# Turning round the one-hot products of an expert-weight matrix: which operand stays, which one moves

## The chip, the cores and the metric

The kernel runs on one core of a Trainium2 chip. The metric is the device time in microseconds (us). Three runs of the kernel before took 2843.61, 2845.25 and 2845.64 us, with 2845.25 us as the median.

## The reference, cut to what matters

The program is one transformer layer for 256 prompt tokens and 64 sample tokens: differential attention, a gated chunk MLP, memory attention, an output projection, and then a PEER layer, in which every token picks 128 of 16384 experts. The change is in the PEER layer, which the reference writes with gathers:

```
s = jnp.einsum('thpc,hpkc->thpk', q, sub_keys)      # two sets of 128 keys per head
s1, i1 = lax.top_k(s[:, :, 0], 16); s2, i2 = lax.top_k(s[:, :, 1], 16)
...                                                 # the best 16 of the 256 sums, per head
g = softmax(top_s)
a = gelu(einsum('td,thkd->thk', xb, expert_u[eidx]))
out = einsum('thk,thkd->td', g * a, expert_v[eidx])
```

An expert's number is first key times 128 plus second key. Each token has 8 heads times 16 picks, so 128 slots, each with a first key, a second key and a weight.

## The kernel before, in words

For the 256 prompt tokens (`DN`) the kernel doesn't gather. It multiplies the tokens with every expert's row of `peer_u` (the pieces `Up`, 128 of them, each two loads of 512 KB and 48 matmuls at line 413), passes the result through Gelu, weights it with a dense matrix G (experts by tokens, nearly all zeros), and multiplies that with every row of `peer_v` (the pieces `Down`). For the 64 sample tokens the rows are gathered by indirect DMAs on POOL (`gathers`, lines 1502 to 1526), 64 gathers of `pur` and 64 of `pvr`, 1 MB each, into two or three buffers; each is used by one DVE instruction of 2048 elements (`dot`, `axpy`).

G is built while the `Up` pieces run, in 32 units of eight tokens (`TU`), one every two or three pieces (`weights_lane`, lines 1339 to 1359). Such a unit is `g_unit` (lines 1447 to 1475). With slots on the 128 partitions, DVE compares an index table `io` (the number i at every place [i, t]) with the tokens' first keys, and again with their second keys: two one-hot tables in bf16, each 128 keys by 8 tokens with the tokens innermost (`oa`). The weight of a slot is kept as three bf16 parts (`w0`, `w1`, `w2`), so that nothing of its 32 bits is lost, and DVE multiplies the second key's one-hot table by each part (`ob`). Then TensorE makes a 128 by 128 block of G for each token: the first key's one-hot rows of this token stay in the array, and the second key's weighted rows move through it, once for each part, summed in PSUM. Token k's rows are `oa[:, 0, :, k]` and `ob[:, j, :, k]`, so both operands are read in steps of eight bf16 elements, 16 bytes. The products of the first two parts are issued at line 1461; the third goes through the helper at line 271 (`mm`). ACT copies four tokens' blocks at a time into `st`, and a DMA on SP's queue writes 16 tokens to DRAM (`gd`), from where `weights_in` loads them after all units are done.

Float32 work goes through a stream: SP's queue loads `raw`, ACT rounds it into `hi`, DVE takes the rest into `lo`, and three float32r matmuls per block follow at line 413. The buffers of this stream are a ring of four to six.

The order of all engines' instructions is fixed when the program is built, by a small planner (class `Plan`, lines 123 to 249). It keeps a clock for each engine, adds a modelled cost for each instruction (`pe_cost`, `act_cost`, `dve_cost`, `pool_cost`), and lets a task issue its next step when the plan's PE clock has reached the time at which its inputs are due. The first two products of a token add 0.067 us each to the plan's PE clock; the third costs what `pe_cost` says for bf16, 0.0133 us and 128 columns at 2.4 per ns, which is 0.067 us too. `dve_cost` counts a bf16 output at half the time per element.

Of the kernel before, what the change touches and what calls it, by code (L numbers as in the profile page):

```python
# [14 lines left out]
BF16 = mybir.dt.bfloat16  # L15
AF = mybir.ActivationFunctionType
ALU = mybir.AluOpType
# [28 lines left out]
TU = 8  # L46
# [17 lines left out]
class Slots:  # L64
# [10 lines left out]
    def take(self):  # L75
        t, i = self.free.pop(0)
        x = self.make(i)
        self.used[id(x)] = (i, x)
        self.plan.touch(x, t, True)
        return x  # L80
# [171 lines left out]
def size(ap):  # L252
    n = 1
    for k in ap.shape[1:]:
        n *= k
    return n
# [34 lines left out]
def pe_cost(op, a, k):  # L291
    n = size(a[2]) / (2.4e3 if op == "matmul" and a[2].dtype == F32R else 0.6e3)
    if op == "matmul" and a[2].dtype == BF16:
        return 0.0133 + size(a[2]) / 2.4e3
    return max(0.107, n + 0.0133) if op == "matmul" else 0.216


# [4 lines left out]
def dve_cost(op, a, k):  # L302
    out = a[0] if a else k["out"]
    n = size(a[1]) if op == "tensor_reduce" else size(k["in_"]) if op == "max" else \
        size(k["in_values"]) if op in ("max_index", "match_replace") else size(out)
    return 0.16 + n / 0.96e3 * (6.2 if op == "reciprocal" else 0.5 if out.dtype == BF16 else 1)


def pool_cost(op, a, k):
# [9 lines left out]
def hybrid_kernel(ctx: ExitStack, tc: tile.TileContext, ins, outs, stop=None):  # L319
    nc = tc.nc  # L320
    plan = Plan()
    act, dve = Engine(plan, "act", nc.scalar, act_cost), Engine(plan, "dve", nc.vector, dve_cost)
    pool, pe = Engine(plan, "pool", nc.gpsimd, pool_cost), Engine(plan, "pe", nc.tensor, pe_cost)
    sync = Engine(plan, "sync", nc.sync, None)
    take, need, mark, spawn, step = plan.take, plan.need, plan.mark, plan.spawn, plan.step
    mm = pe.matmul
# [856 lines left out]
    R = {}  # L1183
# [155 lines left out]
    def weights_lane():  # L1339
        yield from need(*[("dec", i) for i in range(3)])  # L1340
        rtmp.close()
        q = open_pool(gtmp, "gtmp")
        R["io"] = q.tile([128, 128, TU], BF16, name="io")
        pool.tensor_copy(R["io"], cst[:, C_IO:C_IO + 128, None].to_broadcast([128, 128, TU]))
        OA = Slots(plan, q, "oa", [128, 2, 128, TU], BF16, 2)
        OB = Slots(plan, q, "ob", [128, 3, 128, TU], BF16, 2)
        ST = Slots(plan, q, "st", [128, 128, TB], F32, 2)
        st = None
        for t0 in range(0, DN, TU):
            yield from need(("up", GE0 + (GEN - GE0) * t0 // DN))  # L1350
            if t0 % TB == 0:
                st, = yield from take(ST)
            oa, ob = yield from take(OA, OB)
            spawn(g_unit(t0, oa, ob, OA, OB, ST, st))
        while len(gdone) < DN // TU:
            yield
        gtmp.close()
        open_late()
        mark("G")
# [86 lines left out]

    def g_unit(t0, oa, ob, OA, OB, ST, st):

        col = lambda nm: R[nm][:, None, t0:t0 + TU].to_broadcast([128, 128, TU])
        dve.tensor_tensor(oa[:, 0], R["io"], col("k0"), op=ALU.is_equal)  # L1450
        dve.tensor_tensor(oa[:, 1], R["io"], col("k1"), op=ALU.is_equal)
        yield
        for j in range(3):
            dve.tensor_tensor(ob[:, j], oa[:, 1], col(f"w{j}"), op=ALU.mult)
            yield
        for a in range(TU // 4):
            bk, = yield from take(BK)
            for k in range(4 * a, 4 * a + 4):
                o = bk[:, 128 * (k % 4):128 * (k % 4) + 128]
                for j in range(2):  # L1460
                    nc.tensor.matmul(o, oa[:, 0, :, k], ob[:, j, :, k], start=j == 0, stop=False)  # L1461
                    plan.clk["pe"] += 0.067
                mm(o, oa[:, 0, :, k], ob[:, 2, :, k], start=False, stop=True)
            yield
            o = t0 % TB + 4 * a
            act.activation(st[:, :, o:o + 4], bk.rearrange("p (t i) -> p i t", t=4), AF.Copy)
            BK.give(bk)
        OA.give(oa)
        OB.give(ob)
        if o == TB - 4:  # L1470
            plan.see(st)
            yield
            sync.dma_start(gd[t0 // TB][:, :128 * TB], st.rearrange("p i t -> p (i t)"))
            ST.give(st)
        gdone.append(t0)
# [393 lines left out]
```

## Time and profile before

| | us |
|---|---|
| median of three runs | 2845.25 |
| the profiled execution's own time | 2845.33 |
| its span, first to last instruction | 2843.6 |
| time outside the span | 1.7 |
| PE busy | 2788.7 |
| DVE busy | 1870.9 |
| ACT busy | 1101.7 |
| POOL busy | 472.7 |
| bytes moved by DMA | 634.75 MB |

A row of the profile's groups has the line and engine, the operation, the tiles (output, then inputs), the shapes and how often it ran; then the busy time of all in us and the mean of one in ns; then the idle time of the engine before it and what ended it. Matmuls are pipelined: one's duration is longer than its distance from the next, so distances are read from the chain of waits. [...]

The span has three stretches that matter here: everything up to the end of the routing (until 1365 us), the `Up` pieces with the building of G among them (1365 to 2005 us) and their last pieces (to 2104 us), and the `Down` pieces (to 2844 us).

### The profile page before, as it was taken

What the parts mean: (1) busy time and instruction counts of PE and PEld (TensorE: products, weight loads), DVE (VectorE), ACT (ScalarE), POOL (GpSimd) and SP (SyncE); (2) the same over time, 40 slices, a digit from 0 to 9 for tenths busy, and PEclk for the clock granted to TensorE, in tenths of its full rate; (3) what the DMA queues carried; (4) which work ended last, traced back from release to release, by engine and by line L of the source; (5) the groups of instructions that cost most, each with busy time, mean ns of one, the idle gap of its engine ahead of it and who ended that gap; (6) DMA issues with size and microseconds to landing.
All of it is one profiled execution on the core that took longest, in us unless ns stands there. A gap on an engine that the chain in (4) does not pass through costs nothing.

```text
span 2843.6 us, 42779 instructions
## 1 busy us (share of the span) xinstructions
PE 2788.7 (98%) x17350; PEld 2556.7 (90%) x17350; DVE 1870.9 (66%) x2673; ACT 1101.7 (39%) x1449; POOL 472.7 (17%) x459
## 2 busy tenths in 40 slices
PE   7899999999999999999999999999999899999999
PEld 5899899999999999999899989898997787888887
DVE  8446665444445578898655655555678887888884
ACT  4343444333333343454333333333443334344443
POOL 6423431000001231111100010000112120211100
PEclk9899999999999999999888988888999999999999
DMA  7534343444444544668676666676889888899984
GB/s 220 157 116 126 120 129 124 149 149 151 151 151 156 172 153 163 199 224 283 245 260 234 244 246 230 238 243 229 319 296 330 319 321 294 326 366 341 329 288 140
DMA packets 231909, 634.75 MB, mean 223 GB/s; under 512 B 15776, under 2 KB 70048, under 8 KB 213152
## 3 DMA queue, kind: packets, MB, share of 16 engines
q1 hardware_dynamic: 206624, 474.58, 49.9%
q0 software_dynamic: 21056, 142.76, 13.4%
q10 hardware_dynamic: 4032, 14.68, 1.3%
q8 instruction: 136, 2.23, 0.3%
q14 instruction: 61, 0.50, 0.0%
HBM read 594.08 MB, written 37.88 MB: 222 GB/s over the span
## 4 chain that ended last, share of the span: by engine, by line
PE 85%; DVE 3%; DMA 2%; ACT 1%; issue 1%; ACTq 0%; DVEq 0%
PE mm L413 75%; PE bk L271 5%; PE bk L1461 4%; DMA raw<-pv 2%; DVE lo L271 1%; ACT hi L271 1%; DVE x2s L271 1%; DVE xb L271 0%; ACT xb L271 0%; DVE hs L271 0%; DVE x2t L271 0%; DVE e L271 0%; DVE w L271 0%; ACT w L271 0%; DVE vt L271 0%
## 5 line engine op out<-in xcount | busy, mean ns | idle before, releaser
L271 DVE TENSOR_TENSOR lo<-raw,hi 128x1024 fp32r<-128x1024 f32 (+1 forms) x622 | 874.2, 1408 | 815.2 <-ACT hi L271 814.7
L271 ACT ACTIVATE hi<-raw 128x1024 fp32r<-128x1024 f32 (+1 forms) x622 | 731.5, 1177 | 1052.8 <-PE mm L413 841.4
L413 PE MATMUL mm<-xb,hi 128*128 128x256 f32 x4096 | 802.9, 298 | 0.0
L413 PEld LDWEIGHTS mm<-xb,hi 128*128 128x128 f32 x4096 | 686.1, 205 | 6.3
L413 PE MATMUL mm<-x_g,hi 128*128 128x320 f32 x2688 | 605.1, 314 | 0.0
L413 PE MATMUL mm<-xb,lo 128*128 128x256 f32 x2048 | 601.9, 294 | 0.0
L413 PEld LDWEIGHTS mm<-x_g,hi 128*128 128x128 f32 x2688 | 448.8, 189 | 8.3 <-issue 4.1
L413 PEld LDWEIGHTS mm<-xb,lo 128*128 128x128 f32 x2048 | 417.6, 204 | 0.0
L413 PE MATMUL mm<-x_g,lo 128*128 128x320 f32 x1344 | 416.7, 310 | 0.0
L413 PEld LDWEIGHTS mm<-x_g,lo 128*128 128x128 f32 x1344 | 253.7, 189 | 0.0
L413 PE MATMUL mm<-hi,xb 128*128 128x512 f32 x688 | 217.9, 391 | 0.0
L413 PE MATMUL mm<-hi,w 128*128 128x512 f32 x688 | 217.0, 390 | 0.0
L271 POOL DMA_INDIRECT r<-pur,idx x62 | 81.9, 1321 | 681.0 <-DVE r L271 668.0
L1461 PE MATMUL bk<-ob,oa 128*128 128x128 bf16 x512 | 166.9, 416 | 0.0
L413 PEld LDWEIGHTS mm<-hi,xb 128*128 128x128 f32 x688 | 130.0, 189 | 27.0
L413 PEld LDWEIGHTS mm<-hi,w 128*128 128x128 f32 x688 | 129.2, 188 | 27.2 <-issue 0.5
L271 DVE SCALAR_TENSOR_TENSOR r<-r,xs 128x2048 f32<-128x2048 f32 x62 | 141.6, 2284 | 0.0
L413 PE MATMUL mm<-lo,w 128*128 128x512 f32 x344 | 134.3, 390 | 6.0 <-DVE lo L271 6.0
L413 PE MATMUL mm<-lo,xb 128*128 128x512 f32 x344 | 134.8, 392 | 2.7 <-DVE lo L271 2.7
L271 POOL DMA_INDIRECT r<-pvr,idx x44 | 70.6, 1604 | 387.7 <-DVE x2s L271 386.3
L413 PE MATMUL mm<-xb 128*128 128x512 f32 x504 | 122.4, 398 | 9.0 <-ACT xb L271 5.6
L413 PEld LDWEIGHTS mm<-xb 128*128 128x128 f32 x504 | 96.7, 193 | 30.8 <-ACT xb L271 6.5
(272 smaller groups left out, 3602.3 us busy)
## 6 DMA issues: line engine op xcount, KB each, us to landing
raw<-pu SPq DMA_DIRECT2D x256, 512.0 KB, 4.2
raw<-pv SPq DMA_DIRECT2D x128, 1024.0 KB, 7.2
raw<-win SPq DMA_DIRECT2D x168, 512.0 KB, 3.5
raw<-wbr SPq DMA_DIRECT2D x32, 512.0 KB, 3.5
raw<-wout SPq DMA_DIRECT2D x32, 512.0 KB, 3.5
raw<-wq SPq DMA_DIRECT2D x32, 512.0 KB, 3.6
gd<-st SPq DMA_DIRECT2D x16, 1024.0 KB, 6.8
gg<-gd SPq DMA_DIRECT2D x16, 1024.0 KB, 12.6
```

The costliest lines, as they stand in the source:

```text
L271: r = f(*a, **k)
L413: nc.tensor.matmul(o, stays, moves, start=first, stop=last and n == len(products) - 1)
L1461: nc.tensor.matmul(o, oa[:, 0, :, k], ob[:, j, :, k], start=j == 0, stop=False)
```

## The change: what it does

The second key's one-hot table is written with the keys innermost, `[t, i]`, in the same memory (`kb`). The three parts of the weight are multiplied onto the first key's table, which keeps its layout (`ka`). The weighted rows now stay in the array, and the second key's plain rows move, 128 neighbouring elements for each token. The block of G that comes out is the same, first key on the partitions and second key along the row. The number of products and of DVE instructions is the same. DVE's second comparison now reads `io` in steps of eight elements, and the keys as one value repeated 128 times. Two prices of the planner change: a bf16 product costs 0.08 us in place of 0.067, and a bf16 output of DVE counts as half price only where its innermost length is eight.

```
 def pe_cost(op, a, k):
...
     if op == "matmul" and a[2].dtype == BF16:
-        return 0.0133 + size(a[2]) / 2.4e3
+        return 0.08
...
-    return 0.16 + n / 0.96e3 * (6.2 if op == "reciprocal" else 0.5 if out.dtype == BF16 else 1)
+    return 0.16 + n / 0.96e3 * (6.2 if op == "reciprocal" else 0.5 if out.dtype == BF16 and out.ap[-1][1] == TU else 1)
...
     def g_unit(t0, oa, ob, OA, OB, ST, st):
 
+        ka, kb = oa[:, 0], oa[:, 1].rearrange("p i t -> p (i t)").rearrange("p (t i) -> p t i", t=TU)
         col = lambda nm: R[nm][:, None, t0:t0 + TU].to_broadcast([128, 128, TU])
-        dve.tensor_tensor(oa[:, 0], R["io"], col("k0"), op=ALU.is_equal)
-        dve.tensor_tensor(oa[:, 1], R["io"], col("k1"), op=ALU.is_equal)
+        dve.tensor_tensor(ka, R["io"], col("k0"), op=ALU.is_equal)
+        dve.tensor_tensor(kb, R["io"][:, None, :, 0].to_broadcast([128, TU, 128]),
+                          R["k1"][:, t0:t0 + TU, None].to_broadcast([128, TU, 128]), op=ALU.is_equal)
         yield
         for j in range(3):
-            dve.tensor_tensor(ob[:, j], oa[:, 1], col(f"w{j}"), op=ALU.mult)
+            dve.tensor_tensor(ob[:, j], ka, col(f"w{j}"), op=ALU.mult)
             yield
         for a in range(TU // 4):
             bk, = yield from take(BK)
             for k in range(4 * a, 4 * a + 4):
                 o = bk[:, 128 * (k % 4):128 * (k % 4) + 128]
                 for j in range(2):
-                    nc.tensor.matmul(o, oa[:, 0, :, k], ob[:, j, :, k], start=j == 0, stop=False)
-                    plan.clk["pe"] += 0.067
-                mm(o, oa[:, 0, :, k], ob[:, 2, :, k], start=False, stop=True)
+                    nc.tensor.matmul(o, ob[:, j, :, k], kb[:, k], start=j == 0, stop=False)
+                    plan.clk["pe"] += 0.08
+                mm(o, ob[:, 2, :, k], kb[:, k], start=False, stop=True)
             yield
```

## Rows read from the trace of the kernel before

**Rows 1.** The page: busy time and share of the engines, and two lines of its forty slices of the span (PE's granted clock and the DMA engines' busy share, in tenths).
```profile
PE 2788.7 (98%) x17350; PEld 2556.7 (90%) x17350; DVE 1870.9 (66%) x2673; ACT 1101.7 (39%) x1449; POOL 472.7 (17%) x459
...
PEclk9899999999999999999888988888999999999999
DMA  7534343444444544668676666676889888899984
```

**Rows 2.** The page: the chain that ended last, by line, as shares of the span.
```profile
PE mm L413 75%; PE bk L271 5%; PE bk L1461 4%; DMA raw<-pv 2%; DVE lo L271 1%; ACT hi L271 1%; DVE x2s L271 1%; DVE xb L271 0%; ACT xb L271 0%; DVE hs L271 0%; DVE x2t L271 0%; DVE e L271 0%; DVE w L271 0%; ACT w L271 0%; DVE vt L271 0%
```

**Rows 3.** Groups of instructions in the stretch from 1365.4 to 2004.8 us, in which all of G is built.
```profile
L413 PE MATMUL mm<-xb,hi 128*128 128x256 f32 x2277 | 471.5, 309 | 0.0
...
L413 PE MATMUL mm<-xb,lo 128*128 128x256 f32 x1138 | 343.8, 302 | 0.0
...
L271 DVE TENSOR_TENSOR lo<-raw,hi 128x1024 fp32r<-128x1024 f32 x143 | 174.9, 1224 | 262.4 <-ACT hi L271 262.4
L1461 PE MATMUL bk<-ob,oa 128*128 128x128 bf16 x512 | 166.9, 416 | 0.0
...
L271 PE MATMUL bk<-ob,oa 128*128 128x128 bf16 x256 | 105.6, 412 | 0.0
...
L271 DVE TENSOR_TENSOR ob<-oa,r 128x1024 bf16<-128x1024 bf16 x62 | 42.4, 685 | 0.0
L271 DVE TENSOR_TENSOR oa<-io,r 128x1024 bf16<-128x1024 bf16 x62 | 39.9, 684 | 0.0
...
L271 DVE TENSOR_TENSOR ob<-oa,w 128x1024 bf16<-128x1024 bf16 x31 | 21.2, 684 | 0.0
```

**Rows 4.** The chain of waits in order of time, from 1364 to 1374 us: start, length in us, engine, output tile and line, and how many instructions of it.
```profile
1365.58 0.51 PE bk L1461 x2
1366.09 0.23 PE bk L271
1366.32 0.47 PE bk L1461 x2
...
1370.22 0.47 PE bk L1461 x2
1370.69 0.23 PE bk L271
...
1371.62 2.56 PE mm L413 x12
```

**Rows 5.** The longest unbroken pieces of the chain of the whole run, in the same form.
```profile
1328.15 37.43 PE mm L413 x312
...
2004.75 97.03 PE mm L413 x797
...
2417.57 363.33 PE mm L413 x1601
```

**Rows 6.** Busy time in short stretches around two pairs of products: start and end, length, busy us and count for PE, PEld, DVE, ACT and POOL, then PE's granted clock, DMA share and GB/s.
```profile
1367.50:1369.40 1.90, 1.90 (x11) 1.39 (x10) 1.90 (x2) 0.60 (x1) 0.00 (x0) 1.00 0.96 388
1370.10:1371.60 1.50, 1.50 (x8) 1.05 (x7) 0.00 (x0) 0.00 (x0) 0.54 (x1) 0.50 0.97 298
...
1377.00:1382.00 5.00, 5.00 (x44) 5.00 (x44) 2.61 (x3) 2.39 (x3) 0.00 (x0) 1.00 0.66 225
...
1391.00:1393.00 2.00, 2.00 (x11) 2.00 (x11) 0.00 (x0) 0.00 (x0) 0.00 (x0) 0.50 0.86 225
```

**Rows 7.** The same view over whole stages; the lines are from two answers of it.
```profile
1200.00:1300.00 100.00, 100.00 (x842) 100.00 (x840) 92.32 (x150) 53.05 (x72) 13.08 (x15) 1.00 0.67 227
1300.00:1360.00 60.00, 60.00 (x502) 60.00 (x502) 47.93 (x47) 26.87 (x40) 9.63 (x6) 1.00 0.83 301
...
2420.00:2785.00 365.00, 365.00 (x1608) 301.23 (x1606) 310.81 (x296) 150.86 (x132) 47.07 (x30) 1.00 0.91 329
...
1365.40:2004.80 639.40, 639.40 (x4183) 575.88 (x4182) 373.25 (x396) 207.52 (x277) 61.15 (x49) 0.87 0.68 239
2004.80:2103.80 99.00, 99.00 (x816) 99.00 (x816) 66.54 (x66) 43.66 (x60) 15.79 (x11) 0.98 0.87 318
2103.80:2400.00 296.20, 280.39 (x1219) 229.06 (x1218) 238.47 (x222) 113.65 (x100) 51.10 (x29) 0.98 0.89 323
```

**Rows 8.** The instructions of line 1461: duration in ns (least, median, most), first and last start, shapes.
```profile
L1461 PEld LDWEIGHTS <-oa x512: 142/146/170, 1365.4 to 2003.9; 128*128 128x128 bf16 x171
L1461 PE MATMUL bk<-ob,oa x512: 407/413/451, 1365.4 to 2004.1; 128*128 128x128 bf16 x171
```

**Rows 9.** From the groups of the stretch from 1263 to 1365 us, before the products begin: the weight loads of line 413.
```profile
L413 PEld LDWEIGHTS mm<-xb,hi 128*128 128x128 f32 x564 | 88.0, 192 | 0.0
```

**Rows 10.** From the groups of the whole run: a comparison on DVE of 1024 float32 elements, one value repeated along the inner 16.
```profile
L271 DVE TENSOR_TENSOR big<-xt,cst 128x1024 f32<-128x1024 f32 x12 | 14.8, 1232 | 0.0
```

**Rows 11.** Who waited for whom from 1365 to 2005 us: us in total, times, longest.
```profile
POOL r L271 <- DVE r L271: 574.6, 49, 19.8
ACT hi L271 <- PE mm L413: 264.6, 141, 3.7
```

**Rows 12.** DMA issues, count, KB each and median us from issue to landing: the gathers from 1230 to 1370 us, and the gathers from 1370 to 2005 us.
```profile
r<-pur,idx POOLq DMA_INDIRECT x11, 8.6
...
r<-pur,idx POOLq DMA_INDIRECT x49, 6.4
```

## The prediction, written before the changed kernel was run

> **What bounds the kernel now.** I read the page's busy shares first. PE is busy for 2788.7 of 2843.6 us; its granted clock is below full in the middle slices, and the DMA engines have room in just those slices but little after them [rows 1]. Next the chain by line: line 413 holds 75% of it, and line 1461 with line 271, the two lines that issue the products of G, up to 9% more [rows 2]. So PE sets the end, and a microsecond taken from PE counts, as long as nothing else comes late.
>
> The stretch to look at is 1365.4 to 2004.8 us, 639.4 us, where PE never idles [rows 7]. It holds 2277 + 1138 = 3415 matmuls of line 413 and 512 + 256 = 768 products of G [rows 3]. The busy means there (309 and 416 ns) overlap and can't be added; the chain gives the distances. In an unbroken run line 413 takes 37.43 us for 312, 0.120 us each [rows 5]. The products take 0.70 us for three, 0.233 each, and 0.51 + 0.23 + 3 x 0.70 = 2.84 us for a group of twelve [rows 4]. They take the same 0.47 + 0.23 us at 1366 us and at 1370 us [rows 4], though the granted clock was 1.00 up to 1369.4 and 0.50 after 1370.1 [rows 6]. So PE's clock doesn't set their pace, and 128 columns of bf16 take almost twice what 256 columns of line 413 take. What differs is the operand's step: the moving rows are read 16 bytes apart, 1.83 ns for each column.
>
> There is a second loss. [...] At the lower level line 413 takes 2.56 us for 12, 0.213 each [rows 4]. The sum of the stretch: 3415 x 0.120 = 409.8, and 64 groups x 2.84 = 181.8; together 591.6. The remaining 47.8 us is what the lower clock costs line 413.
>
> **The change part by part.**
>
> *Products.* 768 before and after, each with a weight load of its own before and after (512 under line 1461 [rows 8], the others under line 271). Now the moving side is contiguous and the 16-byte step is left on the staying side alone. The new distance is in no row. Below, 0.060: line 413 moves 256 columns in 0.120, so 128 can hardly be faster. Above, 0.233, nothing gained. Between them lies the weight load's own duration, 0.146 median and 0.142 to 0.170 at either clock [rows 8]; the load has this same 16-byte step already now. A load is longer than the room it needs: line 413 goes on every 0.120 us [rows 5] though one of its loads lasts 0.192 [rows 9], so loads overlap by 0.072. Taking that from 0.146 leaves about 0.075, which I take. 768 x 0.075 = 57.6 us; saved 181.8 - 57.6 = 124.2. With 0.060 it is 135.7, with 0.146 it is 69.7.
>
> *Clock.* A pair of groups then lasts 24 x 0.075 = 1.8 us in place of 5.7, and it fell only after some 4 us of them [rows 6]. I take it that the clock stays up: 47.8 us saved. The ends are 0 and 47.8.
>
> *DVE.* One comparison of each unit loses its form with the inner eight contiguous on all sides. It took 0.684 us [rows 3]; the nearest row for 1024 elements at the slower pace is a float32 comparison, 1.232 [rows 10]. 32 x 0.55 = 17.6 us more. DVE's work in the stretch becomes 373.3 + 17.6 = 390.9 us [rows 7]. Hidden: after the savings the stretch lasts 639.4 - 172.0 = 467.4 us, so DVE is 84% busy, against 92% from 1200 to 1300 us, where PE was never short [rows 7]. Behind the comparison DVE has `lo` queued, on which PE waits; today ACT, which makes `hi` ahead of it, itself waits 264.6 us on PE to give buffers back [rows 11], so the ring runs full and 0.55 us is absorbed. Uncovered it would cost 17.6. The three multiplications keep their layout and price.
>
> *ACT, SP, POOL.* Their instructions are the same. ACT needs 207.5 us [rows 7] of the shorter stretch.
>
> *DMA.* The bytes don't change, the time does: 639.4 us at 239 GB/s is 152.8 MB [rows 7], in 467.4 us 327 GB/s. That has been reached with PE whole: 329 GB/s from 2420 to 2785 us. But from 2104 to 2400 us, at 323 GB/s, PE lacked 15.8 of 296 us [rows 7]. So 0 to 5.3% of 467 us is given back, 0 to 25; I take half, 12 us. What is late next is a load of `raw` or a gathered buffer, on which DVE's queue stands.
>
> *The planner.* Its PE clock goes 768 x 0.0133 = 10 us further and DVE's some 17, so tasks fall between other blocks here and there, in the `Down` part too. What this can move is what `Down` loses to its loads of `pv`, 2% of the chain [rows 2], some 57 us. I put it at 0, with a third of that, 20 us, either way as its bounds.
>
> Sum: -124.2 - 47.8 + 12 = -160. From the profiled execution's own 2845.3 us (span 2843.6 and 1.7 around it; the median of the runs, 2845.25, is the same) that gives 2685 us.
>
> [...] The row: a moving operand in 16-byte steps took 1.83 ns a column at either clock [rows 4, 6]. [...]
>
> **The rivals.**
>
> A. Transfers take more back. If the stretch gets no more than the 301 GB/s of 1300 to 1360 us [rows 7], it lasts 152.8 MB / 301 = 508 us, 40 more than PE needs: 2845 - 172 + 40 = 2713, and to 2725 with some of it carried on into `Down`. For it: 0.87 and 0.89 DMA share in the next two stages [rows 7]. Against: 329 GB/s with PE whole.
>
> B. The clock still falls. Products partly at the lower level, near 0.10 each, save 105 us, line 413's 47.8 stay lost, transfers have more room: 2740 to 2745; falling half as often, 2720. Against: the pair is a third as long.
>
> C. The weight load isn't hidden and sets 0.146: 69.7 + 47.8 saved, 2728; with the clock falling as well, 2776. For it: the load's duration; against: loads that overlap at line 413.
>
> D. The change doesn't do what it says: a weight load in 16-byte steps is held as the moving read was, 0.233 each. Products and clock stay as they are, DVE's 17.6 us are hidden: 2845, no change. Against it speaks the load's 0.146.
>
> E. Slower. The gathers set the pace: DVE stands in order at a `dot` whose buffer hasn't landed, `lo` waits behind it, and PE behind that. The stretch has 49 gathers [rows 12]; one every 13 us is today's pace, and above that the kernel is slower, at 14 us by 49 us more, 2894. With two buffers that means 26 us from issue to reuse. Against: they land in 6.4 us, in 8.6 where PE ran whole [rows 12], and POOL waits for DVE, 574.6 us, not for them [rows 11].
>
> **How the numbers follow.** The forecast, 0.62: its own range goes from 2655 (0.060 a product, nothing given back, `Down` a little better) to 2710 (0.085, 25 us given back, `Down` worse by some 8). A 0.15, B 0.10, C 0.08, D 0.03, E 0.02. The range for 8 in 10 takes in the forecast, A and most of B and C: 2655 to 2740. About 0.2%, 5.7 us, is what a measurement of this kernel can tell from no change. Faster: the first four, 0.95; the same: D, 0.03; slower: E, 0.02.
>
> **What would show it.** In the chain, groups of twelve products in about 0.9 us in place of 2.84; moving operand and weight load named the other way round. Granted clock 1.00 through the building of G, and line 413 at 0.120 right behind the products; if it is 0.50 there, B. Products at 0.146 mean C, at 0.233 D. The comparison with `kb` in 1.2 us, and no wait of PE on `lo` in that stretch. DMA at 0.9 share there; waits of ACT on `raw` or of DVE on gathers, tens of us in all, mean A. The stretch shorter by some 160 us and `Down` as long as before; if `Down` has grown by more than 20 us, the order or the transfers are where I was wrong.

## The result and the profile after

The changed kernel takes 2670.34 us (median of four runs, 2668.41 to 2672.79), against 2845.44 us for the kernel before; the ratio is 0.9386, with a 95% interval of 0.937 to 0.9403. The profiled execution has a span of 2666.7 us, 176.9 less than before. The forecast was 2685 us.

The page, in the lines of [rows 1] and [rows 2]:

```profile
PE 2614.2 (98%) x17350; PEld 2443.2 (92%) x17350; DVE 1909.5 (72%) x2673; ACT 1100.1 (41%) x1449; POOL 480.9 (18%) x459
...
PEclk9999999999999999999999999999998999999999
DMA  7533434444444554465889899889989879999964
...
PE mm L413 77%; PE bk L271 4%; DMA raw<-pv 2%; DVE lo L271 1%; PE bk L1463 1%; DVE x2s L271 1%; DVE xb L271 1%; ACT hi L271 1%; DVE x2t L271 1%; DVE hs L271 0%; SPq L271 0%; ACT xb L271 0%; DVE e L271 0%; DVE w L271 0%; ACT w L271 0%
```

PE is still the bound. The dip of PE's granted clock, which is given as a share of its full speed, is gone from the middle slices, and the DMA engines are now as busy there as in the `Down` part. The line of the first two products (1463 now) has gone from 4% of the chain to 1%.

The chain from 1364 to 1374 us, to be read against [rows 4]:

```profile
1365.59 0.18 PE bk L1463 x2
1365.78 0.06 PE bk L271
1365.84 0.12 PE bk L1463 x2
...
1366.40 0.41 PE mm L413 x3
...
1367.59 6.53 PE mm L413 x54
```

Three products take 0.18 to 0.19 us, 0.062 each, where they took 0.70. From its first product to line 413, the first group of twelve lasts 1366.40 - 1365.59 = 0.81 us and the second 0.78; the 52 groups up to 1760 us have a mean of 0.80, where it was 2.84. Right behind the second group line 413 goes on at 6.53/54 = 0.121 us, so the clock has not fallen; over the stretch it is 1.00.

The stages, as in [rows 7]: the stretch in which G is built, the last `Up` pieces, and the beginning of `Down`:

```profile
1365.40:1830.30 464.90, 464.87 (x4194) 461.99 (x4193) 412.44 (x398) 207.76 (x277) 67.70 (x49) 1.00 0.89 329
1830.30:1930.40 100.10, 100.10 (x836) 100.10 (x836) 68.67 (x66) 42.52 (x60) 16.69 (x12) 1.00 0.95 349
1930.40:2220.00 289.60, 272.71 (x1160) 221.71 (x1159) 236.59 (x221) 111.98 (x99) 53.63 (x28) 0.97 0.87 313
```

The stretch has gone from 639.4 to 464.9 us, 174.5 of the 176.9 us. What lies behind it took 2843.6 - 2004.8 = 838.8 us and takes 836.4. In the first part of `Down` PE lacks 16.9 of 289.6 us, against 15.8 of 296.2.

The groups of that stretch, against [rows 3]:

```profile
L413 PE MATMUL mm<-xb,hi 128*128 128x256 f32 x2284 | 419.0, 285 | 0.0
...
L413 PE MATMUL mm<-xb,lo 128*128 128x256 f32 x1142 | 323.1, 283 | 0.0
...
L271 DVE TENSOR_TENSOR lo<-raw,hi 128x1024 fp32r<-128x1024 f32 x144 | 175.2, 1221 | 52.5 <-ACT hi L271 52.5
...
L271 DVE TENSOR_TENSOR oa<-io,r 128x1024 bf16<-128x1024 bf16 x62 | 82.5, 1372 | 0.0
```

The sum on PE: 3426 x 0.120 = 411.1, and 64 x 0.80 = 51.2, together 462.3 of 464.9 us. The remaining 2.6 us stand where line 413 follows a group: its first three take 0.41 us, not 0.36. DVE's comparisons are the surprise: the mean of the two is 1.372 us, and as the first one is unchanged at 0.684, the second takes 2.06 us, not 1.23. DVE is busy 412.4 of 464.9 us, and its idle time ahead of `lo` has shrunk from 262.4 to 52.5 us.

### The profile page after: what moved, and what is told of

It reads as the page before. It is cut to its first block, busy times and chain, and to the rows that moved or that the text cites. A ratio compares the mean times of both kernels' runs of the same rounds, so it can differ in the third digit from the quotient of the medians.

```text
span 2666.7 us, 42780 instructions
## 1 busy us (share of the span) xinstructions
PE 2614.2 (98%) x17350; PEld 2443.2 (92%) x17350; DVE 1909.5 (72%) x2673; ACT 1100.1 (41%) x1449; POOL 480.9 (18%) x459
## 4 chain that ended last, share of the span: by engine, by line
PE 82%; DVE 4%; DMA 2%; issue 1%; ACT 1%; SPq 0%; ACTq 0%; DVEq 0%
PE mm L413 77%; PE bk L271 4%; DMA raw<-pv 2%; DVE lo L271 1%; PE bk L1463 1%; DVE x2s L271 1%; DVE xb L271 1%; ACT hi L271 1%; DVE x2t L271 1%; DVE hs L271 0%; SPq L271 0%; ACT xb L271 0%; DVE e L271 0%; DVE w L271 0%; ACT w L271 0%
## 5 line engine op out<-in xcount | busy, mean ns | idle before, releaser
L413 PE MATMUL mm<-xb,hi 128*128 128x256 f32 x4096 | 747.9, 285 | 0.0
L413 PEld LDWEIGHTS mm<-xb,hi 128*128 128x128 f32 x4096 | 638.5, 192 | 0.0
L413 PE MATMUL mm<-xb,lo 128*128 128x256 f32 x2048 | 579.8, 283 | 0.0
L413 PEld LDWEIGHTS mm<-xb,lo 128*128 128x128 f32 x2048 | 392.9, 192 | 0.0
L271 POOL DMA_INDIRECT r<-pur,idx x62 | 87.7, 1415 | 489.9 <-DVE r L271 468.7
L271 DVE TENSOR_TENSOR xb<-raw,xb 128x2048 fp32r<-128x2048 f32 x42 | 96.2, 2290 | 45.7 <-ACT xb L271 45.7
L413 PE MATMUL mm<-xb,w 128*128 128x512 f32 x504 | 119.8, 392 | 0.7 <-DVE xb L271 0.7
## 6 DMA issues: line engine op xcount, KB each, us to landing
gg<-gd SPq DMA_DIRECT2D x16, 1024.0 KB, 13.1
```

Of the source, the lines that this page charges most:

```text
L271: r = f(*a, **k)
L413: nc.tensor.matmul(o, stays, moves, start=first, stop=last and n == len(products) - 1)
```

## The experiments

Times are medians. The changed kernel took 2670.3 us in the first comparison and 2668.3 in a later one; the kernel before stayed between 2844.1 and 2846.6 in all.

**The planner's prices alone, and the change without them.** The kernel before with the new prices:

```
-        return 0.0133 + size(a[2]) / 2.4e3
+        return 0.08
...
-    ... 0.5 if out.dtype == BF16 else 1)
+    ... 0.5 if out.dtype == BF16 and out.ap[-1][1] == TU else 1)
...
-                    plan.clk["pe"] += 0.067
+                    plan.clk["pe"] += 0.08
```

> The kernel before with nothing but the planner's two new prices (0.08 us for a bf16 product, full price for DVE's bf16 outputs whose innermost length isn't eight). Theory (the products and the clock make the gain): the products stay at 0.233 us and the clock still falls, so the time stays within 10 us of 2845. Rival (the new order of instructions makes part of the gain): 20 us or more below 2845, most of it after 2104 us.

2849.2 us, ratio 1.0013 (1.0003 to 1.0023). The other way round, the changed kernel with these three lines as they were before:

> The changed kernel with the planner's old prices (0.067 us and half price for all bf16 outputs), so that the plan thinks DVE's second comparison cheap. Theory: products at 0.062 us as in the changed kernel, 2670 us within 10. Rival (the prices matter): 20 us or more above 2670, with waits of PE on lo while G is built.

2669.1 us, ratio 0.938 (0.9364 to 0.9395). The order that the planner makes gains nothing: the new prices alone cost the kernel before 4 us, and the changed kernel does without them. The gain is that of the two operands' layout.

**Layout without the turn.** The first key's one-hot rows stay, as before, and the weighted second key's rows move, written keys innermost. The index comes from a dense row (`ir`).

```
-            dve.tensor_tensor(ob[:, j], ka, col(f"w{j}"), op=ALU.mult)
+            dve.tensor_tensor(oc[j], kb, R[f"w{j}"][:, t0:t0 + TU, None].to_broadcast([128, TU, 128]), op=ALU.mult)
...
-                    nc.tensor.matmul(o, ob[:, j, :, k], kb[:, k], start=j == 0, stop=False)
+                    nc.tensor.matmul(o, oa[:, 0, :, k], oc[j][:, k], start=j == 0, stop=False)
```

> The layout without the turn: the first key's one-hot rows stay (16-byte steps, as before), the second key's rows times the weight's parts move, but with keys innermost, so that what moves is contiguous. DVE's second comparison and its three multiplications write rows of 128 keys; the index is read from a dense row. Theory (the moving operand's step alone sets the product's pace): 0.062 us a product as in the changed kernel, clock 1.00. DVE pays for it: three multiplications at about 1.23 in place of 0.684 us, so some 440 of 465 us, and the time is 2670 to 2690. Rival (which operand stays matters): products stay above 0.1 us.

2666.7 us in one run, 3 us below the range stated. The instructions of the tile `oa` (duration in ns, least, median and most):

```profile
L1466 PE MATMUL bk<-ob,oa x512: 223/225/278, 1368.6 to 1831.9; 128*128 128x128 bf16 x171
...
L271 DVE TENSOR_TENSOR ob<-oa,r x64: 1210/1218/1223, 1356.8 to 1823.7; 128x1024 bf16<-128x1024 bf16 x64
```

A product lasts 0.225 us as in the changed kernel (0.226; 0.413 before), and the distance between two is 0.062. So it is not the turn that makes the products short, but that what moves is contiguous. The turn saves DVE work: here the three multiplications cost 1.218 each in place of 0.684 and DVE is busy 433.9 us of the stretch, which the time doesn't show, as PE is busy throughout, 464.6 of 464.6 us.

**The step itself: 8 and 32 bytes in place of 16.** The kernel before with `TU = 4`, which changes the step of both operands:

> The kernel before with units of four tokens in place of eight, so both operands of the products are read in steps of 8 bytes in place of 16; products and columns are the same. [...] Rival (any step beyond neighbouring elements costs the same): 0.233 as before. DVE's pieces are half as long and twice as many, some 10 us more in all, which PE's bound hides. Time: 2845 minus some 88 us for the products and up to 48 for the clock, so 2710 to 2760 under the theory, 2845 under the rival.

The chain, and the instructions of line 1461:

```profile
1365.65 0.24 PE bk L1461 x2
1365.89 0.12 PE bk L271
1366.01 0.23 PE bk L1461 x2
```

```profile
L1461 PEld LDWEIGHTS <-oa x512: 112/117/138, 1365.5 to 1871.6; 128*128 128x128 bf16 x171
L1461 PE MATMUL bk<-ob,oa x512: 282/297/303, 1365.5 to 1871.7; 128*128 128x128 bf16 x171
```

0.35 us for three, 0.118 each: half of 0.233, which is the case of 2710 to 2760 us. Its 88 us for the products were 181.8 - 90.9 = 90.9 in the run. The load's 0.117 doesn't set this, as the changed kernel's longer loads, 0.148, let products go every 0.062. The granted clock stayed at 1.00 through the building of G. The time was 2698.1 us in one run, 12 below that range. The groups took 64 x 1.42 = 90.9 us and nothing was lost behind them, so products and clock make 139 of the 147 us saved; the other 8 lie behind the stretch and were not followed up. Then the kernel before with `TU = 16`, and one buffer in place of two for `oa` and `ob`:

> The kernel before with units of sixteen tokens, so both operands are read in steps of 32 bytes; one buffer each for the tables, as two don't fit, so DVE prepares a unit only after the products of the one before. Measured with 8 bytes: 0.118, with 16: 0.233 a product. [...] Rival (the price grows with the step): about 0.46. Groups of 48 products stand together, so the clock falls at least as long as before; time about 2845 under the theory, 3020 under the rival.

```profile
L1461 PEld LDWEIGHTS <-oa x512: 142/150/173, 1368.6 to 1988.2; 128*128 128x128 bf16 x171
L1461 PE MATMUL bk<-ob,oa x512: 412/423/458, 1368.7 to 1988.5; 128*128 128x128 bf16 x171
```

The chain has these pairs start at 1368.81, 1369.56 and 1370.29, so three products take 0.73 to 0.75, some 0.24 each; the step has doubled and the price has not. The time, 2827.3 in one run, is 18 us below the 2845 that goes with an unchanged product. The stretch:

```profile
1368.60:1988.90 620.30, 620.30 (x4125) 553.55 (x4124) 357.39 (x312) 204.63 (x273) 72.43 (x48) 0.85 0.68 244
```

It holds 4125 - 768 = 3357 matmuls of line 413 and 64 groups of 2.90 us, so 620.3 - 402.8 - 185.6 = 31.9 us were lost to the clock, 16 less than the 47.8 before. The clock is indeed lower on the mean, 0.85 against 0.87; but there are half as many units, each with its four groups side by side, and the products of the later groups still take 0.24. So the lower clock meets less of line 413.

Contiguous 0.062 us (0.056 where both are, below), 8 bytes 0.118, 16 bytes 0.233, 32 bytes 0.24: for each of the 128 columns that is 0.48 ns (0.44), 0.92, 1.82 and 1.9. So from 8 bytes to 16 the price doubles, and from 16 to 32 it hardly grows. Why it stops growing there, these runs don't show. Nor is a step of 8 bytes as good as none: 0.118 us against 0.056 to 0.062.

**The clock by itself.** The kernel before with the two groups of a unit set apart:

```
-            yield
+            for _ in range(1 if a else 20):
+                yield
             o = t0 % TB + 4 * a
```

> The kernel before, with the two groups of twelve products of a unit set some 20 blocks of line 413 apart instead of one. Products stay in 16-byte steps, so 0.233 us each. Theory (the clock falls because a pair of groups keeps PE on slow products for over 4 us): a single group of 2.84 us leaves the clock at 1.00, line 413 stays at 0.120, and the time falls by about 48 us to 2797. Rival (the clock falls by how many products there are, wherever they stand): it falls as often or more, and the time stays within 15 us of 2845 or grows.

2815.4 us, ratio 0.9892 (0.9875 to 0.9908): 30 us, not 48. The stretch, and the chain at its beginning:

```profile
1365.40:1985.00 619.60, 619.60 (x4254) 555.83 (x4253) 377.96 (x399) 207.24 (x281) 58.37 (x48) 0.96 0.71 249
```

```profile
1368.73 7.54 PE mm L413 x63
1376.28 0.51 PE bk L1461 x2
...
1379.12 2.65 PE mm L413 x15
1381.76 0.49 PE bk L1461 x2
```

Products are as slow as before, 0.233 each, and yet the mean clock of the stretch is 0.96 against 0.87. After the first group line 413 runs at 7.54/63 = 0.120; the second group then meets the next unit's first one, only 15 matmuls behind it, and those 15 take 0.177 each. The sum as in the prediction: the stretch holds 4254 - 768 = 3486 matmuls of line 413, and 619.6 - 418.3 - 181.8 leaves 19.5 us for the lower clock, where 47.8 were lost; 28 of the 30 us are this. So the clock's part is a loss of its own, with the products unchanged. With groups of 1.42 us (8-byte steps) and of 0.80 us (the changed kernel) the granted clock stayed at 1.00 over the stretch.

**Where DVE's 2.06 us come from.** The changed kernel, its second comparison reading a dense row:

```
-        dve.tensor_tensor(kb, R["io"][:, None, :, 0].to_broadcast([128, TU, 128]),
+        dve.tensor_tensor(kb, R["ir"][:, None, :].to_broadcast([128, TU, 128]),
```

> The changed kernel with one more small tile, a dense row of 128 indices, from which the second comparison reads in place of 16-byte steps. Theory (the step costs DVE too: 2.05 us in place of 1.23, 16 bytes for each element): the comparison takes about 1.23, DVE's work while G is built falls by 26 us, from 412 to 386. Since PE sets the pace there, the time stays within 5 us of 2670. Rival (2.05 us is the price of the one key repeated 128 times): the comparison stays near 2.05. Second rival (DVE is already late there): the time falls by 10 us or more.

2670.1 us, ratio 0.9378 (0.9366 to 0.9391).

```profile
L271 DVE TENSOR_TENSOR oa<-ir,r x32: 1214/1218/1222, 1355.0 to 1816.7; 128x1024 bf16<-128x1024 bf16 x32
```

1.218 us, so the step of 16 bytes costs DVE 0.84 us over 1024 elements on top of the lost fast form, 1.218 in place of 0.684. DVE's work in the stretch falls to 388.5 us, and the time doesn't move: it was hidden.

**How deep the cover is.** The changed kernel with that comparison issued twice:

> The changed kernel with the second comparison issued twice, to find what DVE's cover is worth: 32 x 2.05 = 66 us more of DVE, 478 us in a stretch of 465. Theory (the one comparison is hidden because DVE has some 50 us to spare): spare time goes first, so the stretch grows by about 13 us or a little more, 2683 to 2700. Rival (each microsecond of DVE there is already paid): 66 us more, 2735. Third case (the cover is larger than it looks): within 5 us of 2670.

2679.5 us, ratio 0.9417 (0.9403 to 0.9432), 9 us more than the changed kernel for some 66 us of DVE. The waits from 1365 to 1840 us:

```profile
PEld L271 <- DVE ob L271: 13.1, 13, 2.0
DVE lo L271 <- ACT hi L271: 12.1, 11, 3.3
```

DVE's idle time ahead of `lo` is used up first, from 52.5 to 12.1 us; then the weight loads wait for `ob`, 13.1 us. It is the theory, though the time is 4 us below its range. The change itself has put 44 us more on DVE (below) and left 52.5, so it uses rather less than half of the cover.

**Do the transfers set the pace now?** The changed kernel without the weight's third part (its multiplication and its product are left out):

```
-        for j in range(3):
+        for j in range(2):
             dve.tensor_tensor(ob[:, j], ka, col(f"w{j}"), op=ALU.mult)
...
-                for j in range(2):
+                for j in range(1):
                     nc.tensor.matmul(o, ob[:, j, :, k], kb[:, k], start=j == 0, stop=False)
...
-                mm(o, ob[:, 2, :, k], kb[:, k], start=False, stop=True)
+                mm(o, ob[:, 1, :, k], kb[:, k], start=False, stop=True)
```

> The changed kernel with two of the weight's three parts (the third part's multiplication and product are left out, so G is less exact). 256 products and 32 multiplications fewer. Theory (PE still sets the pace while G is built, transfers have room): 256 x 0.062 = 16 us less there, 2654. Rival (at 329 GB/s the transfers set the pace): the stretch stays at 465 us or loses under 5, with DVE or ACT waiting for gathers or raw, 2665 to 2670.

2649.1 us, ratio 0.9309 (0.9295 to 0.9323).

```profile
1365.40:1812.00 446.60, 446.60 (x3908) 443.92 (x3907) 387.85 (x361) 204.70 (x275) 64.10 (x47) 1.00 0.90 335
```

```profile
L1463 PE MATMUL bk<-oa,ob x256: 223/226/280, 1360.2 to 1810.9; 128*128 128x128 bf16 x128
```

From the first product to the last it took 450.7 us in place of 464.7, with 12 more matmuls of line 413 (1.4 us) in between, so nearly all of 256 x 0.062 = 16 us, with PE never idle at 335 GB/s. At the end of the run 21 us are gone; the other 5 were not followed up. PE sets the pace; transfers don't yet.

**The weight load's step.** The changed kernel with all five tables keys innermost, the index from a dense row:

```
+        ka, kb, *oc = (x.rearrange("p i t -> p (i t)").rearrange("p (t i) -> p t i", t=TU)
+                       for x in (oa[:, 0], oa[:, 1], ob[:, 0], ob[:, 1], ob[:, 2]))
...
+                    nc.tensor.matmul(o, oc[j][:, k], kb[:, k], start=j == 0, stop=False)
```

> The changed kernel with every table written keys innermost, so that the operand that stays is contiguous too; all five DVE instructions of a unit then take about 1.22 us. Theory (the matmul's own 128 columns set 0.062, the weight load is hidden): products stay at 0.062 us, though the load's duration falls from 0.148 to about 0.11. Rival (the weight load in 16-byte steps sets 0.062): products fall to 0.056 or less, 5 us in all. DVE gains some 43 us over the dense-index kernel, about 431 of 465 us, and hides it: 2665 to 2672.

2659.1 us in one run, and the theory is refuted. The instructions of `ob`, and the chain:

```profile
L1467 PEld LDWEIGHTS <-ob x512: 96/98/99, 1371.3 to 1827.0; 128*128 128x128 bf16 x171
L1467 PE MATMUL bk<-oa,ob x512: 219/219/230, 1371.3 to 1827.0; 128*128 128x128 bf16 x171
```

```profile
1371.44 0.13 PE bk L1467 x2
1371.56 0.06 PE bk L271
1371.62 0.11 PE bk L1467 x2
...
1372.12 0.41 PE mm L413 x3
```

The load lasts 0.098 us in place of 0.148, three products take 0.17, 0.056 to 0.057 each, and a group starts in 0.13 in place of 0.18. So the last 0.006 us of the changed kernel's products were the weight load's step. Timed, beside the changed kernel on the same chip:

> The same kernel with all tables keys innermost, timed. Theory (only the shorter products count: 0.056 in place of 0.062 us and a shorter start of each group, 768 x 0.006 + 64 x 0.05 = 8 us at most): 4 to 10 us under the changed kernel, 2660 to 2666. Rival (its single time of 2659 was chance): the same as the changed kernel within 3 us.

> The changed kernel again, on the same chip and beside the same runs of the kernel before, as the measure for the one with all tables keys innermost: 2668 to 2673.

2659.4 us with all tables keys innermost, ratio 0.9347 (0.9334 to 0.936), and 2668.3 us for the changed kernel, 0.9379 (0.9366 to 0.9392). From its first product to line 413 a group takes 1372.12 - 1371.44 = 0.68 us, 0.69 on the mean, in place of 0.80. That is 64 x 0.11 = 7.0 of the 8.9 us; the rest was not followed up. DVE's extra work (443.4 us of 461.8) is hidden while G is built, where PE is never idle. This version is faster than both kernels.

## Why the prediction was right

The time, 2670, lies in the stated range and in the likeliest case's own range of 2655 to 2710; the saving was 175 us where 160 was forecast. The terms as measured, -130.6 for the products and -45.2 for the clock with nothing given back, come to -175.8. Term by term:

*Products:* 0.075 us was taken, 0.062 measured, so 181.8 - 51.2 = 130.6 us saved in place of 124.2. The cause was named rightly, a 16-byte step on the moving side; the runs with 8 and 32 bytes and the one without the turn show it. The weak step was the weight load: taking line 413's overlap off its 0.146 us gave too much by a fifth. Its overlap is larger here, 0.148 - 0.062 = 0.086. But that the load's step still costs something was right, 0.006 us, by the kernel with all tables dense. That kernel also breaks the lower bound: 128 columns can go every 0.056 us, where 0.060 was taken as the least.

*Clock:* 47.8 us were to come back; 45.2 did, as 2.6 us remain behind the groups at full clock. The kernel with the groups set apart shows it as a term of its own.

*DVE:* 17.6 us more were forecast, and it was 32 x 1.37 = 44 us (DVE's busy time went from 373.3 to 412.4 us; neighbouring instructions overlap a little: the groups of the stretch add up to 439.4 us, for 412.4 busy). The nearest row, a float32 comparison of 1.232 us, was dense; this one also pays for its 16-byte steps, 2.06 us against 1.218 from a dense row. That a price 2.5 times too low did no harm was partly luck. The argument, that DVE has idle time to spare, was right, but its size wasn't known: 52.5 us of it were left, and the run with the comparison doubled shows where it ends.

*Transfers:* 12 us were to be given back, and none were: PE is busy 464.87 of 464.90 us at 329 GB/s. Gathers land later, in 8.5 us in place of 6.4 [rows 12], and still nobody waits for them; POOL waits for DVE:

```profile
r<-pur,idx POOLq DMA_INDIRECT x49, 8.5
```

```profile
POOL r L271 <- DVE r L271: 390.3, 49, 12.9
ACT hi L271 <- PE mm L413: 208.6, 128, 2.9
DVE lo L271 <- ACT hi L271: 52.5, 52, 3.3
```

This was the one term taken as half of a loss seen elsewhere, in `Down`. That loss belongs to `Down`, where it is as large as before; the rate alone doesn't make it.

*The planner:* put at 0 with 20 us either way; the new prices cost the kernel before 4 us, and the changed kernel without them takes the same within its spread (2669.1, against 2670.3 and 2668.3).

Of the rivals, A fell with the 0.89 DMA share at which PE was never idle, B with the clock of 1.00, C with 0.062 us against the load's 0.148. D, a weight load held at 0.233, fell too, but half of its idea is true: in 16-byte steps the load lasts 0.148, dense 0.098. E needs gathers that are late, and there are none.

## What to carry to other kernels

Lay out the operand that moves through the array so that its columns are neighbours: with bf16 in steps of 16 bytes, 128 columns took 0.233 us, almost four times the 0.062 of the dense form, and PE showed as busy all the while, 639.4 of 639.4 us. Judge TensorE by the distance between instructions in the chain, not by busy time, and ask of each slow group what it does to the granted clock of the work behind it: here 0.50 in place of 1.00, and line 413 at 0.213 us in place of 0.120. Where a layout has to be strided for somebody, give it to the side that hides it (here the weight load, whose 16-byte steps cost 0.006 us a product), and then check that engine's own price for the step.

## What the runs showed that was not expected

The pace of products in 16-byte steps is the same at both clock levels, 0.70 us for three at 1.00 and at 0.50 [rows 4, 6], and the price hardly grows beyond that step: 0.118 us at 8 bytes, 0.233 at 16, 0.24 at 32. The duration of a weight load is much less sensitive and levels off there too: 0.098 dense, 0.117 at 8 bytes, 0.148 at 16, 0.150 at 32. DVE pays as well, 2.06 us in place of 1.218 for 1024 elements with one input in steps of 16 bytes, so the strided comparison costs three times the 0.684 us of the form that it replaced.
